# Gate and up projections by seven block products, with sums of weights on VectorE, and down products placed between them

## The chip, the cores and the metric

The kernel runs on one core of a Trainium2 chip. A core has TensorE for matmuls, VectorE, ScalarE and GpSimd for work on elements, and queues that move data; SyncE's queue brings in all weights here. The metric is the device time of one execution in microseconds. Each engine takes its instructions in order and waits on semaphores where it needs another engine's result.

## The reference

A decoder trunk of two layers runs over one sequence of 512 tokens, width 1024. Each layer is a feed-forward step with half weight, an attention (stick-breaking in the first layer, sliding window in the second), and a second feed-forward step; each begins with an RMS norm. All is float32.

```python
def swiglu(h, w_gate_up, w_down):
    gate, up = jnp.split(h @ w_gate_up, 2, axis=-1)
    return (jax.nn.silu(gate) * up) @ w_down
...
    x = x + 0.5 * swiglu(rms_norm(x, norm_gains[i, 0]), ffn_w_gate_up[i, 0], ffn_w_down[i, 0])
    h = rms_norm(x, norm_gains[i, 1])
    ...
    x = x + 0.5 * swiglu(rms_norm(x, norm_gains[i, 2]), ffn_w_gate_up[i, 1], ffn_w_down[i, 1])
```

The inner width of a feed-forward layer is 2816, 22 columns of 128 for gate and as many for up.

## The kernel before, in words

The work is six stages, "0s12w3": FFN0, stick-breaking attention, FFN1, FFN2, window attention, FFN3. The state x lies transposed in eight tiles of 128 features by 512 tokens. A float32 product is made from numbers split into a high and a low part: `terms` (with `mm`, L77) issues three matmuls per tile of 128 x 128 weights, high by high, high by low, low by high. The low part of x is made in `norm_tile` (ScalarE L255, VectorE L256).

Weights come in units of 128 x 1024 (512 KB) into three raw buffers. ScalarE casts a unit to its high part (L183), then VectorE subtracts to get the low part (L188); there are three buffers for split weights, and a unit's buffer is opened again when its last matmul has read it. The order of units is fixed by `queue`.

A feed-forward stage first runs all 22 columns of gate and up: per column two units, each 8 x 3 matmuls of 512 tokens into one bank. Then `swiglu` multiplies both by `rbc`, the inverse norm of each token broadcast to all partitions (L308, L310), applies silu on ScalarE (L309), multiplies (L311) and splits the result (L314, L315). After the last column, eight outputs of 22 x 3 matmuls follow (`dn`); each is added into x (L301) and normed for the next stage.

`rbc` is made while the first units run. After the first unit `norm_rows` sums the squares on TensorE (`ss`) and VectorE computes `nv` and then `nr` by three rounds of small operations on 128 x 4. After the second unit `norm_bcast` spreads it: ScalarE and VectorE make diagonals (`dgh`, `dgl`, L294), two matmuls make `bc`, and VectorE copies it to `rbc` (L298).

Only TensorE's instructions keep the order in which the code is written:

```python
self.scalar, self.vector, self.gpsimd, self.sync = nc.scalar, nc.vector, nc.gpsimd, nc.sync
self.tensor = _Ordered(tc, nc.tensor)
```

A scheduler fixes the order on the other engines when the program is built, by when it reckons the inputs are there; on the chip each engine then keeps to it.

Of the kernel before, what the change touches and what calls it, by code (L numbers as in the profile page):

```python
# [15 lines left out]
P = 128  # L16
# [6 lines left out]
DOWN = (8, 7, 7)  # L23
# [85 lines left out]

class _Trunk:  # L110
    def __init__(self, tc, pools, psum, aps):
        self.tc, self.nc = tc, _Engines(tc)
        self.const, self.work = pools
        self.psum = psum
        self.aps = aps
        self.units = []
        self.raw, self.ready = [], []
        self.taken = self.spent = 0
        self.roped = False
        self.extra = -1  # L120
# [8 lines left out]
    def terms(self, out, pairs, first=True, last=True, release=()):  # L129

# [3 lines left out]
        for i, ((wh, wl), (xh, xl)) in enumerate(pairs):  # L134
# [27 lines left out]
    def _open(self, n):
        size = self.units[n][1]
        hi = self.work.tile([P, size], F32R, tag="whi", name=f"whi{n}", bufs=UNITS)
        lo = self.work.tile([P, size], F32R, tag="wlo", name=f"wlo{n}", bufs=UNITS)
        self.ready.append((hi, lo))

    def advance(self, hi, lo):

        n = self.extra = len(self.ready)  # L170
        self.ready.append((hi, lo))
        self._part(n)
        self._load()

    def _part(self, n, i=0, pieces=1):
        nc, (ap, size, pool) = self.nc, self.units[n]
        size //= pieces
        s = slice(i * size, (i + 1) * size)
        hi, lo = self.ready[n]
        raw = self.raw[n]  # L180
        if pieces > 1:
            nc.sync.dma_start(raw[:, s], ap[:, s])
        nc.scalar.copy(hi[:, s], raw[:, s])  # L183
        if pool and pieces == 1:
            for t in (slice(0, size // 2), slice(size // 2, size)):
                nc.gpsimd.tensor_sub(lo[:, t], raw[:, t], hi[:, t])  # L186
        else:
            nc.vector.tensor_sub(lo[:, s], raw[:, s], hi[:, s])  # L188

    def release(self, count):  # L190
        self.spent += count
        ahead = UNITS + (self.spent <= self.extra)
        while count and len(self.ready) < min(self.spent + ahead, len(self.units)):
            n = len(self.ready)
            self._open(n)
            self._part(n)
            self._load()

    def weights(self, a):

        hi, lo = self.ready[self.taken]
        self.taken += 1
        h3, l3 = (t.rearrange("p (a b) -> p a b", a=a) for t in (hi, lo))
        return [(h3[:, i, :], l3[:, i, :]) for i in range(a)]


    def setup(self, which):
# [823 lines left out]
```

## Time and profile before

| | us |
|---|---|
| median of 3 runs shown (1910.4 to 1915.54) | 1911.14 |
| the profiled execution | 1910.23 |
| its span | 1908.4 |
| FFN1, gate/up (634.10 to 875.09) | 240.99 |
| FFN1, down (875.09 to 994.77) | 119.68 |
| FFN2, gate/up (994.77 to 1235.54) | 240.77 |
| FFN2, down (1235.54 to 1355.30) | 119.76 |

The span runs from the first instruction to the last on the core; the execution's own time has 1.8 us around it. The limits of the stretches are the starts and ends of pieces in the chain of work that ended last. In such a chain each piece is followed by what it released; where it stays on one engine for hundreds of instructions, that engine set the time there. An engine's busy share is of the whole span; the table by stretches gives it for one stage. In rows of a timeline the bracket at the end is the engine's idle time ahead of the instruction and who ended it. Matmuls overlap, so the time of one in a timeline is longer than the distance between two starts.

### The profile page before, as it was taken

What the parts mean: (1) busy time and instruction counts of PE and PEld (TensorE: products, weight loads), DVE (VectorE), ACT (ScalarE), POOL (GpSimd) and SP (SyncE); (2) the same over time, 40 slices, a digit from 0 to 9 for tenths busy, and PEclk for the clock granted to TensorE, in tenths of its full rate; (3) what the DMA queues carried; (4) which work ended last, traced back from release to release, by engine and by line L of the source; (5) the groups of instructions that cost most, each with busy time, mean ns of one, the idle gap of its engine ahead of it and who ended that gap; (6) DMA issues with size and microseconds to landing.
All of it is one profiled execution on the core that took longest, in us unless ns stands there. A gap on an engine that the chain in (4) does not pass through costs nothing.

```text
span 1908.4 us, 22581 instructions
## 1 busy us (share of the span) xinstructions
PE 1877.3 (98%) x8994; PEld 1562.6 (82%) x8994; DVE 970.3 (51%) x1535; ACT 695.6 (36%) x1071; POOL 172.3 (9%) x131
## 2 busy tenths in 40 slices
PE   9999999999999999999999999999998999999999
PEld 7888888877887888888888888888887888888887
DVE  7444433378887644443335444432588664444322
ACT  5322222266665333222223332222357542233221
POOL 1000001233320000000100000001142210000000
PEclk9999999999999999999999999999999999999999
DMA  5323333321122322333333223333221022223331
GB/s 168 98 100 100 94 94 93 106 67 56 46 66 67 100 89 99 100 97 92 98 100 98 90 100 100 94 91 102 82 67 34 28 95 99 93 96 99 97 117 62
DMA packets 49929, 170.52 MB, mean 89 GB/s; under 512 B 5920, under 2 KB 6176, under 8 KB 49824
## 3 DMA queue, kind: packets, MB, share of 16 engines
q1 hardware_dynamic: 49824, 169.07, 28.0%
q8 instruction: 71, 1.16, 0.2%
q14 instruction: 34, 0.28, 0.0%
HBM read 166.96 MB, written 2.10 MB: 89 GB/s over the span
## 4 chain that ended last, share of the span: by engine, by line
PE 85%; DVE 7%; issue 4%; ACT 3%; POOL 1%; DMA 0%; SPq 0%; ACTq 0%; DVEq 0%; POOLq 0%
PE gu L77 49%; PE dn L77 23%; PE op L77 4%; PE tok L77 3%; DVE keep L460 2%; PE pv L77 1%; DVE beta L461 1%; DVE qs L377 1%; PE q L77 1%; DVE wt L483 1%; PE sc L77 1%; PE z L77 1%; ACT keep L454 1%; PE ptr L77 0%; DVE e L793 0%
## 5 line engine op out<-in xcount | busy, mean ns | idle before, releaser
L183 ACT CAST whi<-raw 128x1024 fp32r<-128x1024 f32 (+2 forms) x323 | 330.3, 1023 | 949.3 <-issue 358.0
L77 PE MATMUL gu<-xh,whi 128*128 128x512 f32 x1400 | 545.5, 390 | 1.2 <-ACT whi L183 1.2
L77 PE MATMUL gu<-xh,wlo 128*128 128x512 f32 x1400 | 545.0, 389 | 0.7 <-DVE wlo L188 0.7
L77 PE MATMUL gu<-xl,whi 128*128 128x512 f32 x1400 | 544.8, 389 | 0.5 <-DVE xl L256 0.5
L188 DVE TENSOR_TENSOR wlo<-raw,whi 128x1024 fp32r<-128x1024 f32 (+2 forms) x293 | 349.1, 1192 | 239.6 <-ACT whi L183 236.7
L77 PEld LDWEIGHTS gu<-xh,whi 128*128 128x128 f32 x1400 | 262.9, 188 | 56.2 <-ACT whi L183 1.8
L77 PEld LDWEIGHTS gu<-xh,wlo 128*128 128x128 f32 x1400 | 262.8, 188 | 56.0 <-DVE wlo L188 1.9
L77 PEld LDWEIGHTS gu<-xl,whi 128*128 128x128 f32 x1400 | 262.9, 188 | 55.6 <-DVE xl L256 0.9
L77 PE MATMUL dn<-hh,whi 128*128 128x512 f32 x704 | 273.9, 389 | 0.0
L77 PE MATMUL dn<-hl,whi 128*128 128x512 f32 x704 | 273.9, 389 | 0.0
L77 PE MATMUL dn<-hh,wlo 128*128 128x512 f32 x704 | 273.9, 389 | 0.0
L310 DVE TENSOR_TENSOR u<-gu,rbc 128x512 f32<-128x512 f32 x87 | 60.1, 691 | 274.7 <-PE gu L77 274.7
L77 PEld LDWEIGHTS dn<-hh,whi 128*128 128x128 f32 x704 | 132.1, 188 | 27.7
L77 PEld LDWEIGHTS dn<-hh,wlo 128*128 128x128 f32 x704 | 132.1, 188 | 27.4
L77 PEld LDWEIGHTS dn<-hl,whi 128*128 128x128 f32 x704 | 132.1, 188 | 27.2
L308 DVE TENSOR_TENSOR g<-gu,rbc 128x512 f32<-128x512 f32 x88 | 60.8, 691 | 176.5 <-PE gu L77 176.4
L264 POOL TENSOR_TENSOR acc<-acc,sq 128x512 f32<-128x512 f32 x30 | 46.6, 1553 | 1106.0 <-ACT sq L263 1106.0
L186 POOL TENSOR_TENSOR wlo<-raw,whi 128x512 fp32r<-128x512 f32 x60 | 87.5, 1483 | 163.7 <-ACT whi L183 163.7
L77 PE MATMUL tok<-whi,xh 128*128 128x256 f32 x288 | 85.9, 298 | 0.0
L77 PE MATMUL tok<-whi,xl 128*128 128x256 f32 x288 | 81.9, 284 | 0.1
L77 PE MATMUL tok<-wlo,xh 128*128 128x256 f32 x288 | 81.8, 284 | 0.1
L301 DVE SCALAR_TENSOR_TENSOR x<-dn,x 128x512 f32<-128x512 f32 x32 | 22.1, 692 | 110.9 <-PE dn L77 110.9
(310 smaller groups left out, 1950.3 us busy)
## 6 DMA issues: line engine op xcount, KB each, us to landing
raw<-in_gu_dram SPq DMA_DIRECT2D x173, 512.0 KB, 3.3
raw<-in_dn_dram SPq DMA_DIRECT2D x64, 448.0 KB, 3.3
raw<-in_dn_dram SPq DMA_DIRECT2D x32, 512.0 KB, 3.5
raw<-in_sbqk_dram SPq DMA_DIRECT2D x16, 512.0 KB, 3.4
raw<-in_swin_dram SPq DMA_DIRECT2D x10, 512.0 KB, 3.5
raw<-in_sbv_dram SPq DMA_DIRECT2D x8, 512.0 KB, 3.3
raw<-in_sbo_dram SPq DMA_DIRECT2D x8, 512.0 KB, 3.5
raw<-in_swo_dram SPq DMA_DIRECT2D x8, 512.0 KB, 3.4
```

The costliest lines, as they stand in the source:

```text
L77: return self._tc.keep_in_program_order(method(*args, **kwargs))
L183: nc.scalar.copy(hi[:, s], raw[:, s])
L186: nc.gpsimd.tensor_sub(lo[:, t], raw[:, t], hi[:, t])
L188: nc.vector.tensor_sub(lo[:, s], raw[:, s], hi[:, s])
L264: (nc.gpsimd if k < POOL_SQUARES else nc.vector).tensor_add(self.acc, self.acc, sq)
L301: self.nc.vector.scalar_tensor_tensor(self.x[n], ps, factor, self.x[n], ALU.mult, ALU.add)
L308: nc.vector.tensor_mul(g, gu[0], self.rbc)
L310: nc.vector.tensor_mul(u, gu[1], self.rbc)
L377: nc.vector.tensor_sub(out[other, h, :], src[own, :], out[own, h, :])
L454: nc.scalar.activation(keep[:, :, :n], z[:, :, :n], AF.Sigmoid, scale=-0.125)
L460: nc.vector.tensor_tensor_scan(rev, rev, rev, 1.0, ALU.mult, ALU.bypass)
L461: nc.vector.tensor_mul(beta[:, :, : n - 1], beta[:, :, : n - 1], keep[:, :, 1:n])
```

## The change

Gate and up of one column are taken as one product of a 2 x 2 block matrix of weights with a 2 x 2 block matrix of inputs: the weight blocks are gate and up by odd and even tiles of the 1024 features, the input blocks are odd and even tiles by the first and the second 256 tokens. Winograd's form of Strassen's scheme makes it with seven products (`seven`, p from 1 to 7) for eight. Each is 4 tiles x 3 matmuls of 256 columns. Four of the seven read sums of x (`sums_of_x`, made once at each stage's start: four tiles t0 to t3 by ScalarE and VectorE), and four read sums of weights, S1 to S4, which VectorE makes for each column from the raw units (L329, L333, L334). S1 S3 and S2 S4 fill a split buffer each, A22 A11 one, A12 half of one. The first two columns (`PLAIN`) stay as they were, since `rbc` and the sums of x come with them.

The down product is cut by `GROUPS` into six groups of columns (3, 3, 4, 4, 4, 4). A group's eight pieces (one per output tile, a bank of its own, added into x by L471) run between the products of the next group's columns; `ffn_steps` writes that order. The last group's eight pieces come at the end, and only they are followed by the norm. Within a feed-forward stage there are two more raw buffers, two more split ones (`slotx`) and two half ones. The bank names a, b, c hold the products, dn the pieces.

```diff
-DOWN = (8, 7, 7)
+W2 = T // 2
+HALF = KD // 2
+UNIT = KD * P
+PLAIN = 2
+GROUPS = (3, 3, 4, 4, 4, 4)
+MORE_RAWS, MORE_SLOTS, HALF_SLOTS = 2, 2, 2
+HELD = 8
...
+def ffn_steps():
+    steps = [("plain", u) for u in range(2 * PLAIN)]
+    f, last = PLAIN, None
+    for g, size in enumerate(GROUPS):
+        ends = sum(GROUPS[: g + 1])
+        pieces = [("down", g - 1, n) for n in range(KD)] if g else []
+        while f < ends:
+            here = [pieces.pop(0) for _ in range(-(-len(pieces) // (ends - f)))]
+            col = [("seven", p, f) for p in (1, 5, 2, 6, 3, 7, 4)]
+            if last is not None:
+                col.insert(2, last)
+                last = None
+            if not here:
+                last = col.pop()
+            else:
+                col.insert(-1, here.pop())
+                if here:
+                    col.insert(-3, here.pop())
+                while here:
+                    col.insert(-1, here.pop())
+            steps += col
+            f += 1
+    assert last is None
+    return steps + [("down", len(GROUPS) - 1, n) for n in range(KD)]
...
+    def _split(self, n, s=slice(None), load=None):
+        nc = self.nc
+        tiles, kind, reads, pool, _, _ = self.plan[n]
+        hi, lo = (a[:, s] for a in self.ready[n])
+        raws = [self.raws[m] for m in reads]
+        if kind in ("unit", "A22 A11"):
+            src = raws[0][:, s]
+            reads = reads[:1]
+        elif kind == "A12":
+            src = raws[1][:, UNIT // 2 :]
+            reads = reads[1:]
+        else:
+            g, u = (r.rearrange("p (h c) -> p h c", h=2) for r in raws)
+            if kind == "S1 S3":
+                self.sums = self.fp.tile([P, 2, UNIT // 2], F32, tag="sums", name="sums", bufs=1)
+                nc.vector.tensor_add(self.sums, g, u[:, 0:1, :].broadcast_to([P, 2, UNIT // 2]))
+                src = self.sums.rearrange("p h c -> p (h c)")
+            else:
+                nc.vector.tensor_add(u[:, 0, :], self.sums[:, 0, :], g[:, 1, :])
+                nc.vector.tensor_add(u[:, 1, :], u[:, 0, :], u[:, 1, :])
+                src = raws[1]
+        if load is not None:
+            nc.sync.dma_start(src, load)
+        nc.scalar.copy(hi, src)
+        if pool:
+            for h in (slice(0, UNIT // 2), slice(UNIT // 2, UNIT)):
+                nc.gpsimd.tensor_sub(lo[:, h], src[:, h], hi[:, h])
+        else:
+            nc.vector.tensor_sub(lo, src, hi)
...
+    def sums_of_x(self):
+        nc, fp = self.nc, self.fp
+        self.ts = []
+        for m in range(HALF):
+            xg = fp.tile([P, 2, 2, W2], F32, tag="hs", name="xg", bufs=HELD)
+            for i in range(2):
+                k = 2 * m + i
+                g = self.gain[:, self.which * KD + k : self.which * KD + k + 1]
+                nc.scalar.activation(xg[:, i].rearrange("p h t -> p (h t)"), self.x[k], AF.Copy, scale=g)
+            t = fp.tile([P, 4, W2], F32, tag="hs", name="t", bufs=HELD)
+            nc.vector.tensor_sub(t[:, 0, :], xg[:, 0, 0, :], xg[:, 0, 1, :])
+            nc.vector.tensor_sub(t[:, 2, :], xg[:, 1, 1, :], xg[:, 0, 1, :])
+            nc.vector.scalar_tensor_tensor(t[:, 1, :], t[:, 0, :], -1.0, xg[:, 1, 1, :], ALU.mult, ALU.subtract)
+            nc.vector.scalar_tensor_tensor(t[:, 3, :], t[:, 1, :], -1.0, xg[:, 1, 0, :], ALU.mult, ALU.subtract)
+            ts = fp.tile([P, 2, 4, W2], F32R, name=f"t{m}")
+            nc.scalar.copy(ts[:, 0], t)
+            nc.vector.tensor_sub(ts[:, 1], t, ts[:, 0])
+            self.ts.append(ts)
...
+    def seven(self, p, f, tiles):
+        nc, fp = self.nc, self.fp
+        nm = {2: "b", 5: "c", 3: "c"}.get(p, "a")
+        if (nm, f) not in self.cells:
+            tag, bufs = {"a": ("tr", 2), "b": ("pv", 1), "c": ("z", 1)}[nm]
+            self.cells[nm, f] = self.psum.tile([P, T], F32, tag=tag, name=nm, bufs=bufs)
+        ps = self.cells[nm, f][:, :W2]
+        first = p in (1, 2, 5)
+        for m, (n, i) in enumerate(tiles):
+            wh, wl, used = self.tile(n, i)
+            xh, xl = self.operand(p, m)
+            for j, (l, r) in enumerate(((wh, xh), (wh, xl), (wl, xh))):
+                nc.tensor.matmul(
+                    ps, l, r, start=(first and m == j == 0), stop=(m == HALF - 1 and j == 2), skip_group_check=not first,
+                )
+        if p in (1, 6, 5):
+            r = self.cells[f"r{p}", f] = fp.tile([P, W2], F32, tag=f"r{p}", name=f"r{p}", bufs=2)
+            nc.scalar.copy(r, ps)
+        elif p == 2:
+            g = self.cells["g", f] = fp.tile([P, T], F32, tag="g", name="g", bufs=2)
+            nc.vector.tensor_add(g[:, :W2], ps, self.cells["r1", f])
+        elif p == 3:
+            g = self.cells["g", f]
+            nc.vector.tensor_add(g[:, W2:], ps, self.cells["r6", f])
+            nc.vector.tensor_mul(g, g, self.rbc)
+            nc.scalar.activation(g, g, AF.Silu)
+            nc.vector.tensor_mul(g, g, self.rbc)
+        elif p == 7:
+            h = self.cells["h", f] = fp.tile([P, T], F32, tag="h", name="h", bufs=2)
+            nc.vector.tensor_add(h[:, W2:], ps, self.cells["r5", f])
+            nc.vector.tensor_mul(h[:, W2:], h[:, W2:], self.cells["g", f][:, W2:])
+        else:
+            h = self.cells["h", f]
+            nc.vector.tensor_mul(h[:, :W2], ps, self.cells["g", f][:, :W2])
+            self.keep(f, h)
+            for key in [k for k in self.cells if k[1] == f]:
+                del self.cells[key]
+        self.used(n, HALF)
...
+            self.plain(steps[: 2 * PLAIN], first)
+            last = len(GROUPS) - 1
+            tail = [s for s in steps if s[0][:2] == ("down", last)]
+            for step, tiles in steps[2 * PLAIN : len(steps) - len(tail)]:
+                if step[0] == "seven":
+                    self.seven(step[1], step[2], tiles)
+                    if rope and step[1:] == (7, NF // 2):
+                        self.rope_tables()
+                else:
+                    self.down(step[2], step[1], tiles, None)
+            banks = {}
+            for n in range(2):
+                banks[n] = self.bank("dn")
+                self.down_terms(banks[n], last, tail[n][1][:-1], 0)
             for n in range(KD):
+                self.down(n, last, tail[n][1], following, banks.get(n))
...
+    def plain(self, steps, first):
+        xs = list(zip(self.xh, self.xl))
+        banks = {}
+        if first:
+            order = [(k, u) for k in range(HALF) for u in range(UNITS)] + [(k, u) for u in range(UNITS) for k in range(HALF, KD)]
+            order += [(k, UNITS) for k in range(KD)]
+        else:
+            order = [(k, u) for u in range(2 * PLAIN) for k in range(KD)]
+        for k, u in order:
+            if u not in banks:
+                banks[u] = self.psum.tile([P, T], F32, tag="z", name="gu", bufs=1) if u == UNITS else self.bank("gu")
+            self.mm3(banks[u], [(self.tile(*steps[u][1][k]), xs[k])], first=(k == 0), last=(k == KD - 1))
+            if (u, k) == ((1, KD - 1) if first else (0, KD - 1)):
+                self.norm_rows()
+            if (u, k) == ((UNITS, 4) if first else (1, KD - 1)):
+                self.norm_bcast()
+            if k == KD - 1 and u == (3 if first else 1):
+                self.swiglu(0, (banks[0], banks[1]))
+                self.sums_of_x()
+            if k == KD - 1 and u == 3:
+                self.swiglu(1, (banks[2], banks[3]))
+    def down_terms(self, ps, g, tiles, at):
+        f0 = sum(GROUPS[:g])
+        for j, (n, i) in enumerate(tiles, at):
+            self.mm3(ps, [(self.tile(n, i), self.hs[f0 + j])], first=(j == 0), last=(j == GROUPS[g] - 1))
+    def down(self, n, g, tiles, following, ps=None):
+        at = GROUPS[g] - 1 if ps is not None else 0
+        ps = self.bank("dn") if ps is None else ps
+        self.down_terms(ps, g, tiles[at:], at)
+        self.residual(n, ps, -0.5)
+        if following:
+            following(n)
```

The order of instructions follows in three places. The first is VectorE at the start of FFN2, from the fifth step behind the sum of squares (`ss`) on; `raw` is a unit as loaded, `slot` (before: `whi`, `wlo`) its two parts, `sums` the sums S1 S3. Before:

```order
L273 TENSOR_TENSOR nt<-nt,nv 128x4
L188 TENSOR_TENSOR wlo_7523<-raw_7429,whi_7522 128x1024
L274 SCALAR_TENSOR_TENSOR nr<-nt,nr 128x4
L272 SCALAR_TENSOR_TENSOR nt<-nr 128x4
L273 TENSOR_TENSOR nt<-nt,nv 128x4
L274 SCALAR_TENSOR_TENSOR nr<-nt,nr 128x4
L272 SCALAR_TENSOR_TENSOR nt<-nr 128x4
L273 TENSOR_TENSOR nt<-nt,nv 128x4
L274 SCALAR_TENSOR_TENSOR nr<-nt,nr 128x4
L294 SCALAR_TENSOR_TENSOR dgl<-ident,nr,dgh 128x128 x4
L298 COPY rbc<-bc 128x512
```

The change, from the same step on:

```order
L443 TENSOR_TENSOR nt<-nt,nv 128x4
L329 TENSOR_TENSOR sums<-raw_9730,raw_9777 128x1024
L343 TENSOR_TENSOR half_9833<-raw_9777,half_9833 128x512
L444 SCALAR_TENSOR_TENSOR nr<-nt,nr 128x4
L333 TENSOR_TENSOR raw_9777<-sums,raw_9730 128x512
L343 TENSOR_TENSOR slot_9828<-sums,slot_9828 128x1024
L442 SCALAR_TENSOR_TENSOR nt<-nr 128x4
L334 TENSOR_TENSOR raw_9777<-raw_9777 128x512
L443 TENSOR_TENSOR nt<-nt,nv 128x4
L329 TENSOR_TENSOR sums<-rawx_9816,rawx_9821 128x1024
L444 SCALAR_TENSOR_TENSOR nr<-nt,nr 128x4
L343 TENSOR_TENSOR half_10013<-rawx_9821,half_10013 128x512
```

Between the small steps on 128 x 4 stand now sums, a half split and whole splits; before, one split stood there.

The second is VectorE in the middle of FFN2 before, one column:

```order
L310 TENSOR_TENSOR u_8240<-gu_8208,rbc_7589 128x512
L311 TENSOR_TENSOR u_8240<-g_8239,u_8240 128x512
L188 TENSOR_TENSOR wlo190_8234<-raw190_8134,whi190_8233 128x1024
L315 TENSOR_TENSOR hl9_8246<-u_8240,hh9_8245 128x512
L308 TENSOR_TENSOR g_8311<-gu_8249,rbc_7589 128x512
L188 TENSOR_TENSOR wlo191_8275<-raw191_8165,whi191_8274 128x1024
```

The change, in a column of FFN0 with two down pieces (x2 and x3 receive them):

```order
L548 TENSOR_TENSOR g_3153<-c_3125,r6_3167 128x256
L549 TENSOR_TENSOR g_3153<-g_3153,rbc_387 128x512
L343 TENSOR_TENSOR slot95_3252<-rawx57_2949,slot95_3252 128x1024
L551 TENSOR_TENSOR g_3153<-g_3153,rbc_387 128x512
L471 SCALAR_TENSOR_TENSOR x2_113<-dn_3185,x2_113 128x512
L554 TENSOR_TENSOR h_3211<-a_3110,r5_3138 128x256
L555 TENSOR_TENSOR h_3211<-h_3211,g_3153 128x256
L343 TENSOR_TENSOR slot96_3259<-raw58_3081,slot96_3259 128x1024
L471 SCALAR_TENSOR_TENSOR x3_114<-dn_3214,x3_114 128x512
L343 TENSOR_TENSOR slotx93_3227<-sums_3228,slotx93_3227 128x1024
L558 TENSOR_TENSOR h_3211<-a_3110,g_3153 128x256
L343 TENSOR_TENSOR slot97_3264<-raw59_3083,slot97_3264 128x1024
```

A column's row of six operations has become some eighteen, of which a dozen are shown; the split of `slotx93` from `sums` stands behind a residual and another split.

The third is TensorE between two units of gate/up before:

```order
L77 MATMUL gu_1164<-xl7_206,whi25_1086 128x512
L77 MATMUL gu_1164<-xh7_205,wlo25_1087 128x512
L77 MATMUL gu_1205<-xh0_136,whi26_1117 128x512
L77 MATMUL gu_1205<-xl0_137,whi26_1117 128x512
L77 MATMUL gu_1205<-xh0_136,wlo26_1118 128x512
```

The change, from the second down piece of a column of FFN0 to the next column's first product:

```order
L85 MATMUL dn_3214<-hs14_2463,slotx91_3102 128x512 x3
L85 MATMUL dn_3214<-hs15_2613,slotx91_3102 128x512 x3
L85 MATMUL dn_3214<-hs16_2781,slotx91_3102 128x512 x3
L85 MATMUL dn_3214<-hs17_2931,slotx91_3102 128x512 x3
L85 MATMUL a_3110<-t0_423,slot87_2946 128x256 x3
L85 MATMUL a_3110<-t1_434,slot87_2946 128x256 x3
L85 MATMUL a_3110<-t2_445,slot87_2946 128x256 x3
L85 MATMUL a_3110<-t3_456,slot87_2946 128x256 x3
L85 MATMUL a_3269<-xh0_133,slotx92_3107 128x256
```

A piece of four terms, then p4 of the column, then p1 of the next; twelve matmuls of p1 on, p5 reads `slotx93`, which takes the place of `slotx91`, read last by the piece shown.

## Rows read from the trace of the kernel before

**Rows 1.** The page: busy us and shares by engine; the chain's shares by line.
```profile
PE 1877.3 (98%) x8994; PEld 1562.6 (82%) x8994; DVE 970.3 (51%) x1535; ACT 695.6 (36%) x1071; POOL 172.3 (9%) x131
...
PE gu L77 49%; PE dn L77 23%; PE op L77 4%; PE tok L77 3%; DVE keep L460 2%; PE pv L77 1%; DVE beta L461 1%; DVE qs L377 1%; PE q L77 1%; DVE wt L483 1%; PE sc L77 1%; PE z L77 1%; ACT keep L454 1%; PE ptr L77 0%; DVE e L793 0%
```

**Rows 2.** The chain in order of time: start us, us, what it was.
```profile
30.71 2.04 PE gus L77 x9
...
382.99 11.53 PE tok L77 x96
...
875.09 119.68 PE dn L77 x528
994.77 5.44 PE gu L77 x24
1000.21 0.79 PE ss L77 x8
...
1007.06 228.48 PE gu L77 x1008
```

**Rows 3.** Two stretches of FFN2: length, busy us (count) by engine, clock, DMA.
```profile
994.77:1235.54 240.77, 240.77 (x1067) 199.47 (x1067) 114.40 (x149) 73.62 (x94) 0.00 (x0) 1.00 0.30 96
1235.54:1355.30 119.76, 119.76 (x531) 99.18 (x531) 39.53 (x43) 33.10 (x40) 8.03 (x6) 1.00 0.33 99
```

**Rows 4.** Groups of instructions by line and form: busy, mean ns, idle before.
```profile
L188 DVE TENSOR_TENSOR wlo<-raw,whi 128x1024 fp32r<-128x1024 f32 x223 | 274.6, 1232 | 140.3 <-ACT whi L183 140.1
L183 ACT CAST whi<-raw 128x1024 fp32r<-128x1024 f32 x253 | 266.1, 1053 | 711.5 <-issue 358.0 <-PE gu L77 267.1 <-PE dn L77 57.5
...
L310 DVE TENSOR_TENSOR u<-gu,rbc 128x512 f32<-128x512 f32 x87 | 60.1, 691 | 274.7 <-PE gu L77 274.7
...
L77 PEld LDWEIGHTS tok<-wlo,xh 128*128 128x128 f32 x288 | 55.3, 192 | 0.4 <-POOL wlo L186 0.3
...
L756 DVE TENSOR_TENSOR q<-tok,qgain 128x256 f32<-128x256 f32 x16 | 6.6, 416 | 6.4 <-ACT qsq L755 6.3
```

**Rows 5.** Timeline of VectorE at FFN2's start: start us, us, instruction, idle before.
```profile
1001.03 0.16 DVE L282 TENSOR_SCALAR nv<-ss 128x4 f32<-128x4 f32 x1 [2.88 <-PE ss L77]
...
1001.84 0.16 DVE L273 TENSOR_TENSOR nt<-nt,nv 128x4 f32<-128x4 f32 x1
1001.91 1.23 DVE L188 TENSOR_TENSOR wlo<-raw,whi 128x1024 fp32r<-128x1024 f32 x1
1003.06 0.15 DVE L274 SCALAR_TENSOR_TENSOR nr<-nt,nr 128x4 f32<-128x4 f32 x1
1003.25 0.16 DVE L272 SCALAR_TENSOR_TENSOR nt<-nr 128x4 f32<-128x4 f32 x1
...
1004.23 0.16 DVE L274 SCALAR_TENSOR_TENSOR nr<-nt,nr 128x4 f32<-128x4 f32 x1
1004.93 1.23 DVE L294 SCALAR_TENSOR_TENSOR dgl<-ident,nr,dgh 128x128 fp32r<-128x128 f32 x4 [0.53 <-ACT dgh L293]
1007.09 0.69 DVE L298 COPY rbc<-bc 128x512 f32<-128x512 f32 x1 [0.94 <-PE bc L77]
1007.70 1.22 DVE L188 TENSOR_TENSOR wlo<-raw,whi 128x1024 fp32r<-128x1024 f32 x1
1008.84 0.68 DVE L308 TENSOR_TENSOR g<-gu,rbc 128x512 f32<-128x512 f32 x1
1009.44 0.68 DVE L310 TENSOR_TENSOR u<-gu,rbc 128x512 f32<-128x512 f32 x1
```

**Rows 6.** Timeline of ScalarE behind FFN2's first unit.
```profile
1000.06 1.05 ACT L183 CAST whi<-raw 128x1024 fp32r<-128x1024 f32 x1 [3.28 <-issue]
```

**Rows 7.** TensorE's timeline in the stick-breaking stage; then a stretch behind it.
```profile
472.26 0.73 PE L77 MATMUL z<-ks,qs 128*128 128x512 f32 x2 [1.44 <-ACT beta L456]
...
473.00:478.00 5.00, 5.00 (x18) 3.74 (x17) 3.99 (x6) 4.34 (x7) 1.03 (x1) 0.66 0.02 3
```

**Rows 8.** Timeline of VectorE at FFN0's start.
```profile
21.20 0.69 DVE L264 TENSOR_TENSOR acc<-acc,sq 128x512 f32<-128x512 f32 x1 [0.70 <-ACT sq L263]
...
24.01 0.16 DVE L282 TENSOR_SCALAR nv<-ss 128x4 f32<-128x4 f32 x1 [0.64 <-PE ss L77]
```

More of the change, by code (lines that the diff above doesn't have):

```diff
@@ L168, in advance @@
[L168 to L204, printed above, removed]
+    def queue(self, ap, pool=False, special=False):
+        n = len(self.loads)
+        self.loads.append((ap, None))
+        self.reads.append(1)
+        self.plan.append((KD, "unit", (n,), pool, None, special))
@@ new lines, in _ring, with _load @@
+    def _ring(self, rings, free, own):
+        best = None
+        for r in rings if own and own == self.stage else rings[:1]:
+            e = r.evicts()
+            if e is None:
+                return r
+            if free(e) and (best is None or e < best.evicts()):
+                best = r
+        return best
+    def _load(self):
+        n = len(self.raws)
+        r = self._ring(self.raw_rings, lambda e: self.reads[e] == 0, self.loads[n][1])
+        if r:
+            self.raws.append(r.take(n, [P, UNIT], F32))
+        return r
@@ new lines, in advance, with used, tile @@
+    def advance(self, hi, lo):
+        n = len(self.ready)
+        assert self.plan[n][5] and self.plan[n][2][0] < len(self.raws)
+        self.ready.append((hi, lo))
+        self.left.append(self.plan[n][0])
+        self._split(n)
+        self.pump()
+    def used(self, slot, tiles):
+        self.left[slot] -= tiles
+        if tiles and not self.left[slot]:
+            self.pump()
+    def tile(self, slot, i, width=1):
+        hi, lo = (a[:, i * P : (i + width) * P] for a in self.ready[slot])
+        return hi, lo, (slot, width)
@@ L207, in setup, with take @@
+    def take(self, count, width=1):
+        out = []
+        for _ in range(count):
+            n, i = self.at
+            out.append(self.tile(n, i, width))
+            self.at = (n, i + width) if i + width < self.plan[n][0] else (n + 1, 0)
+        return out
     def setup(self, which):
@@ L402, in project_pair @@
             ps = self.bank(nm)
-            yield from self.terms(ps, list(zip(self.weights(KD), xs)), release=1)
+            yield from self.terms(ps, list(zip(self.take(KD), xs)))
             if start:
@@ L531, in project_early @@
         for n in range(UNITS):
-            opened.append([self.bank("op"), self.weights(KD), 0])
+            opened.append([self.bank("op"), self.take(KD), 0])
         while True:
```

287 lines of the change are left out of this document (174 added, 113 removed).

## The prediction

> **What bounds the kernel now.** I read the page's busy shares first. TensorE is busy for 1877.3 of 1908.4 us, 98%, and VectorE for half of them [rows 1]. The page's chain of waits names the lines: matmuls of gate and up make 49% of the span and those of down 23% [rows 1], so the four feed-forward layers (FFN0 to FFN3), where all of the change lies, are bound by TensorE. The long chain gives the pace of its pieces: 1008 matmuls of 512 columns take 228.48 us and 528 of the down part 119.68, both 0.2267 us each [rows 2]. The same chain holds a stretch of 96 matmuls of 256 columns in 11.53 us, 0.1201 each [rows 2]; all 96 are the same three-product form that the change uses. Then the table by stretches: in FFN2's gate/up, VectorE works 114.40 of 240.77 us and ScalarE 73.62, in its down part 39.53 of 119.76 [rows 3]. So VectorE has room on average, and the question is whether it has it where the change puts its work.
>
> **What goes from TensorE.** A column of gate/up was 2 x 8 x 3 = 48 matmuls of 512, 48 x 0.2267 = 10.88 us. By seven products it is 7 x 4 x 3 = 84 of 256, 84 x 0.1201 = 10.09. That is 0.79 less; 20 columns in 4 layers make -63.3 us. The down products are as many and as wide as before: per column 24 x 0.2267 = 5.44 us, now between the products (4.08 in the columns that do group 1, pieces of three over four columns). Between two widths of matmul I count no gap, since the chain runs from the broadcast's 512 columns into the 256 ones without a piece of its own for a wait.
>
> The trace shows a weight load of 128 x 128 at 192 ns, longer than the 120 ns from one 256-column matmul to the next [rows 4], so loads and matmuls overlap further than by one pair, and the pace of rows 2 holds in spite of it. The Trainium skill, page "TensorE: Matmul & The Clock Gate", section "Back-to-back issue gap", has a sustained spacing of about 81 ns for 128 columns and 131 for 512, hence a fixed part that a narrower matmul does not shrink; an estimate by a straight line between gives 98 ns for 256, so 84 x 98 = 8.2 us for a column against 48 x 131 = 6.3, dearer by 1.9, or +155 us in all. The trace does not agree on either end: 227 ns for 512, and 120 for 256, little over half.
>
> **What VectorE and ScalarE get in the steady part.** From start to start an operation of 1024 columns takes VectorE 1.14 us (the split at 1007.70, next start 1008.84) and one of 512 columns 0.605 (1008.84 to 1009.44) [rows 5]; one of 256 is 0.416 long against 0.691 for 512 [rows 4], less the same overlap of 0.085, 0.33. A column with a full share of down holds 5 of 1024 (three splits of gate/up weights, one of a down unit, one sum), 8 of 512 (a half split, two sums, two products, hs, two residuals) and 5 of 256: 5.7 + 4.84 + 1.65 = 12.2 us, or 13.8 by whole durations (5 x 1.232 + 8 x 0.691 + 5 x 0.416). TensorE takes 10.09 + 5.44 = 15.53, and 14.17 where pieces have three terms and VectorE correspondingly less. It stays TensorE's, with 12% to spare. ScalarE's casts are 4.5 of 1.053 [rows 4] a column and its other work about as much again shorter, some 7 us.
>
> One wait is tight. In every second column with two down pieces, the buffer for S1 S3 is the one that the second piece has just left; behind it on TensorE stand p4 and the next p1, 24 x 0.1201 = 2.88 us, and then p5 reads it. A cast that waits for a matmul begins about 0.15 us before the chain's end of that matmul (1000.06 against 994.77 + 5.44) [rows 2, 6]; 1.05 for the cast and 1.23 for the subtraction bring it to 2.1. About 0.7 us is left, and on VectorE a residual and a finished split stand just ahead, on ScalarE another cast. Two more ends matter: p4 waits for VectorE's reading of bank a (L554), and a piece of 2.72 us covers that. I count 0 to +15 us for all of it, taking little (0), because both engines have their work queued earlier; behind a late subtraction stand p4's product and hs, which only the down pieces of the next group read.
>
> **What the layers' starts cost.** Here the work is bunched. Take FFN2, times from its first matmul, 994.77. The sum of squares is done and `nv` begins at 6.26 (1001.03) [rows 5]. Before, the chain of small operations and one split were done at 1004.39, 3.4 us on, the broadcast came out of the way at 1007.09 - 994.77 = 12.3, and TensorE never stopped. Now that chain has between its steps two sums and two splits of 1024 and six operations of 512. A small one followed by a dependent one costs 0.20, by a wide one 0.07 (1001.84 to 1001.91) [rows 5]: 0.8 + 0.6 + 4 x 1.14 + 6 x 0.605 = 9.6, so `nr` ends near 15.2. `dgl` starts 0.55 later, and from its start to `rbc` the row gives 2.16: `rbc` at 18.0. TensorE stands at the broadcast, after two units and the sum, at 11.67, and goes on at about 17.5: a stall near 5.7 that was not there.
>
> From 18.0 VectorE owes: `rbc`, g, h and the product (four of 512, with a dependence of 0.2 each), hs after ScalarE's cast, to 22.0; then 16 of 256 (5.3), the four subtractions for t0 to t3 of 1024 (4.6), two splits (2.3) and g and h of column 1 (1.2): 13.4 more, 35.5, and 36.3 to 37.5 with ScalarE's casts between. p5, the second product, reads t3 last, so it ends 3 matmuls after, at 37.9 at most. By TensorE's work alone it would end at 4 x 5.44 + 0.79 + 0.48 + 24 x 0.1201 = 25.9. I take **+12.0**; with no wait at all VectorE's sum is 28.5 from 6.26, which gives +9. Nothing gives this back, since behind it TensorE is the busier engine in each column.
>
> An idle TensorE also loses its clock. At 472.26 it resumes after 1.44 us idle [rows 7], and in the five us from 473 the granted clock averages 0.66 [rows 7], down to the lower level, 1.2 GHz: 5 x 0.34 = 1.7 us. The stall at the broadcast hides its own in the next; the second one's remains: +1.7. FFN2 and FFN3 then cost 13.7 each. FFN1: thirty small operations of the rope table have moved into the same stretch, at 0.07 to 0.20 (2.1 to 6); I take 2.6, so 16.3.
>
> FFN0: VectorE's last sum of squares starts at 21.20 and `nv` at 24.01 [rows 8]. Now two splits, two sums' halves, a sum, a half split and a split stand ahead of `nv` (4 x 1.14 + 3 x 0.605 = 6.4, so 28.3), and three of 1024 and three of 512 within the chain (6.6, to 34.9). `rbc` 2.7 later, 37.6; two columns' eight operations of 512, a split and their waits to 45; x's sums, an hs and a weight sum 11.6 and some 1.5 for ScalarE: t3 at 58.2, p5's end at 58.6. The fourth unit ended at 30.71 + 2.04 = 32.75 [rows 2]; p1 and p5 behind it end at 35.6. That is +23.1, and with the clock 24.8; without any wait +18.5.
>
> **The sum.** Starts: 24.8 + 16.3 + 2 x 13.7 = **+68.5** (47 without waits and clock, 80 with the longer ends). Products: -63.3. Steady waits: 0. Net +5.2 on the profiled execution's 1910.23 gives 1915.4; the median of the runs shown is 0.9 higher, 1911.14, so **1916**. About 0.3%, 5.7 us, is the least that the measurement tells from no change: below 1905.4 is faster, above 1916.9 slower. This forecast lies at that edge; its own range is 1904 to 1928 (starts 57 to 80).
>
> **Rivals.** *A: the weight buffers' turn becomes the bound.* If ScalarE and VectorE serve the S1 S3 buffer in their queues' order, one cast and one wide operation late (1.05 + 1.14 - 0.7 = 1.5), then each of some eight places a layer stops TensorE by 1.5 us, and one more of the kind per column is possible at bank a: 32 x 1.5 = 48 at most, less when only some miss; +20 to +40 above my sum, 1935 to 1955. It decides from 0.7 us of lateness on. For it: the window of 2.88 us against 2.1, engines that work in order. Against: 12% spare on VectorE. 0.2.
>
> *B: the starts cost about half.* If the sums and splits ahead of `nr` are done in the time VectorE waits for `nv` (2.88 us of idle time before it) [rows 5] and the sums of x run while TensorE is still on its third and fourth units, the stall is 5 to 7 in FFN1 to FFN3 and 12 in FFN0: +30 to +35, so 1911.1 - 63.3 + 33 = 1881, and 1880 to 1904 over its spread. For it: the rings are two units deeper, so sums could be due earlier. Against: the order of the instructions is fixed and puts them behind `nv`, and VectorE's sum alone is +9 a layer. 0.27.
>
> *C: seven products are no cheaper.* If the weight load of 192 ns set the pace where three loads in a row differ, a column would be 84 x 0.192 = 16.1 us, +5.2 on before, over 400 us slower. The 256-column stretch has the same loads and denies it: 0.02. A fixed part of the spacing, as the skill's section has it, is the same rival in a milder form and is in that 0.02.
>
> **How the numbers follow.** Forecast 0.51, A 0.2, B 0.27, C 0.02. The forecast's own part falls 0.05 faster, 0.21 same, 0.25 slower; B 0.26 faster, 0.01 same; A and C slower. Together faster 0.31, same 0.22, slower 0.47. The range leaves B's far end and A's far end out: 1888 to 1944.
>
> **What would show it.** Right: in the timeline of FFN2's start, `rbc` 17 to 19 us after the first matmul, an idle TensorE of 5 to 6 us before the broadcast and another before p5 by VectorE's L511, the granted clock at half behind them, and then columns of 15.5 us without gaps; TensorE's busy time down by some 60 us. Wrong: if TensorE's idle time in a steady column is over 0.5 us, with p5's weight load waiting for L343 or L338, it is A; if the first p5 of FFN2 ends before 32, it is B; if 84 matmuls take over 10.5 us without idle time at the full clock, it is C.

## The result and the profile after

The changed kernel takes 1916.88 us (median of 12 runs, 1910.77 to 1918.65) against 1912.07 before (12 runs, 1910.40 to 1915.54): a ratio of 1.0021, 95% interval 1.0012 to 1.0030. Forecast were 1916 and +5.2 on the kernel before; measured is +4.8 between the medians, and +6.6 between the two profiled executions (1916.84 against 1910.23). That is 0.2% slower, clear of the noise, but within the prediction's bound of 0.3% for no change, the outcome to which it gave 0.22, the least of the three.

Two large terms lie behind this small difference. First the page of the changed kernel, busy us by engine, answering to [rows 1]: TensorE is busy for 35 us less, VectorE for 554 more.

```profile
PE 1842.2 (96%) x11874; PEld 1667.3 (87%) x11874; DVE 1524.5 (80%) x2487; ACT 944.9 (49%) x1511; POOL 170.8 (9%) x131
```

Three columns with a full share of down (one each of FFN1, FFN2 and FFN3), as in [rows 3]: length, busy us of TensorE, weight loads, VectorE, ScalarE, GpSimd, then clock, DMA share, GB/s.

```profile
800.07:815.63 15.56, 15.56 (x109) 14.58 (x109) 12.62 (x19) 7.12 (x10) 0.00 (x0) 1.00 0.33 106
1157.46:1173.02 15.56, 15.56 (x110) 14.58 (x109) 12.55 (x19) 7.12 (x10) 0.00 (x0) 1.00 0.33 106
1709.93:1725.49 15.56, 15.56 (x110) 14.58 (x109) 12.66 (x19) 7.11 (x10) 0.00 (x0) 1.00 0.33 105
```

A column of 15.53 us was forecast, with 12.2 to 13.8 on VectorE and some 7 on ScalarE. TensorE has no gap in it. In the chain (start, length, what), p7 with the next p1 is one piece of 24 matmuls, 0.120 us each; the first in each layer closes its start:

```profile
64.28 2.88 PE a L85 x24
...
642.29 5.44 PE gu L85 x24
...
686.51 2.88 PE a L85 x24
...
1001.38 5.44 PE gu L85 x24
...
1043.90 2.88 PE a L85 x24
...
1551.24 5.44 PE gu L85 x24
...
1596.37 2.88 PE a L85 x24
```

By TensorE's work alone it would come 4 x 5.44 + 0.79 + 0.48 + 60 x 0.1201 = 30.2 us after the first matmul. It comes after 44.2, 42.5 and 45.1: 14.0, 12.3 and 14.9 lost. In FFN0 it would stand at 32.75 + 7.2 = 40.0 and stands at 64.28: 24.3. Together 65.5 us are lost at the starts; the products gain 63.3.

Where TensorE waits at the starts of FFN0 (the first two rows), FFN1, FFN2 and FFN3 (its timeline; the bracket is the idle time and who ended it). In FFN0 six more waits of 0.6 to 1.1 us follow within p5, for ScalarE's casts or VectorE's subtractions of the sums of x:

```profile
37.99 0.79 PE L85 MATMUL bc<-dgh,onesr 128*128 128x512 f32 x1 [6.64 <-ACT dgh L463]
...
49.12 0.58 PE L85 MATMUL c<-t,slot 128*128 128x256 f32 x1 [4.08 <-ACT t L510]
...
659.00 0.80 PE L85 MATMUL bc<-dgh,onesr 128*128 128x512 f32 x1 [4.88 <-ACT dgh L463]
...
678.97 2.90 PE L85 MATMUL c<-t,slot 128*128 128x256 f32 x12 [5.51 <-DVE h L490]
...
1018.09 0.79 PE L85 MATMUL bc<-dgh,onesr 128*128 128x512 f32 x1 [4.88 <-ACT dgh L463]
...
1036.43 2.06 PE L85 MATMUL c<-t,slot 128*128 128x256 f32 x12 [2.63 <-DVE h L490]
...
1567.95 0.79 PE L85 MATMUL bc<-dgh,onesr 128*128 128x512 f32 x1 [4.88 <-ACT dgh L463]
...
1587.68 2.90 PE L85 MATMUL c<-t,slot 128*128 128x256 f32 x12 [4.13 <-DVE h L490]
```

Some 42 of the 65.5 us are idle time. The rest, some 23 us, is the lower clock behind the stalls: there the matmuls take longer and TensorE counts as busy. So its busy time in the four layers falls by 38.2 us (1448.2 to 1410.1) and not by the 63.3 of the products. All of FFN2, for which [rows 3] have the two parts before, 360.53 us of length and of TensorE together:

```profile
1001.38:1358.78 357.40, 349.89 (x2316) 323.24 (x2316) 291.69 (x430) 168.85 (x242) 7.20 (x5) 0.99 0.30 98
```

The VectorE side of FFN2's start, answering to [rows 5]:

```profile
1007.64 0.17 DVE L452 TENSOR_SCALAR nv<-ss 128x4 f32<-128x4 f32 x1 [0.38 <-PE ss L85]
...
1008.44 0.16 DVE L443 TENSOR_TENSOR nt<-nt,nv 128x4 f32<-128x4 f32 x1
1008.52 1.22 DVE L329 TENSOR_TENSOR sums<-raw,raw 128x1024 f32<-128x1024 f32 x1
1009.65 0.68 DVE L343 TENSOR_TENSOR half<-raw,half 128x512 fp32r<-128x512 f32 x1
1010.26 0.15 DVE L444 SCALAR_TENSOR_TENSOR nr<-nt,nr 128x4 f32<-128x4 f32 x1
...
1016.51 0.15 DVE L444 SCALAR_TENSOR_TENSOR nr<-nt,nr 128x4 f32<-128x4 f32 x1
...
1019.35 0.69 DVE L468 COPY rbc<-bc 128x512 f32<-128x512 f32 x1 [0.93 <-PE bc L85]
...
1035.61 0.68 DVE L490 SCALAR_TENSOR_TENSOR h<-gu,rbc 128x512 f32<-128x512 f32 x1
1036.21 1.21 DVE L511 TENSOR_TENSOR t<-t,t 128x1024 fp32r<-128x1024 f32 x1
```

The small steps stand 0.7 to 1.8 us apart where most stood 0.2 apart; `rbc` starts 18.0 us after the layer, t3 is done 36.0 us after it, and between `nv` and there VectorE idles for little over 2 us.

### The profile page after: what moved, and what is told of

Read it like the earlier page. It is cut to its first block, busy times and chain, and to the rows that moved or that the text cites. A ratio compares the mean times of both kernels' runs of the same rounds, so it can differ in the third digit from the quotient of the medians.

```text
span 1915.0 us, 29636 instructions
## 1 busy us (share of the span) xinstructions
PE 1842.2 (96%) x11874; PEld 1667.3 (87%) x11874; DVE 1524.5 (80%) x2487; ACT 944.9 (49%) x1511; POOL 170.8 (9%) x131
## 4 chain that ended last, share of the span: by engine, by line
PE 80%; DVE 13%; issue 3%; ACT 3%; DMA 1%; POOL 0%; SPq 0%; ACTq 0%; DVEq 0%; POOLq 0%
PE dn L85 25%; PE a L85 24%; PE c L85 12%; PE b L85 6%; PE op L85 4%; PE tok L85 3%; PE gu L85 2%; DVE keep L722 2%; DVE beta L723 1%; PE pv L85 1%; DVE slot L343 1%; DVE qs L635 1%; DVE t L511 1%; DVE wt L745 1%; ACT keep L716 1%
## 5 line engine op out<-in xcount | busy, mean ns | idle before, releaser
L85 PE MATMUL dn<-hs,slot 128*128 128x512 f32 x1152 | 279.7, 391 | 0.0
L85 PE MATMUL a<-t,slot 128*128 128x256 f32 x1872 | 249.9, 283 | 0.0
L85 PEld LDWEIGHTS a<-t,slot 128*128 128x128 f32 x1872 | 241.5, 192 | 6.5
L85 PEld LDWEIGHTS dn<-hs,slot 128*128 128x128 f32 x1152 | 211.0, 188 | 40.4
L338 ACT CAST slot<-raw 128x1024 fp32r<-128x1024 f32 (+1 forms) x155 | 160.0, 1033 | 152.2 <-PE a L85 55.2
L85 PE MATMUL dn<-hs,slotx 128*128 128x512 f32 x960 | 233.1, 391 | 0.0
L85 PEld LDWEIGHTS dn<-hs,slotx 128*128 128x128 f32 x960 | 175.7, 188 | 33.4
L343 DVE TENSOR_TENSOR slot<-raw,slot 128x1024 fp32r<-128x1024 f32 (+1 forms) x125 | 155.3, 1243 | 10.8 <-ACT slot L338 10.7
L471 DVE SCALAR_TENSOR_TENSOR x<-dn,x 128x512 f32<-128x512 f32 x192 | 131.5, 685 | 36.6 <-PE dn L85 36.3
L85 PE MATMUL a<-t,slotx 128*128 128x256 f32 x1008 | 134.1, 283 | 0.0
L85 PE MATMUL b<-xh,half 128*128 128x256 f32 x640 | 131.9, 288 | 0.0
L434 POOL TENSOR_TENSOR acc<-acc,sq 128x512 f32<-128x512 f32 x30 | 44.2, 1472 | 818.8 <-ACT sq L433 818.8
L85 PE MATMUL c<-t,slot 128*128 128x256 f32 x576 | 83.5, 295 | 21.0 <-DVE h L490 12.3
```

What stands on the lines that cost most here:

```text
L85: return self._tc.keep_in_program_order(method(*args, **kwargs))
L338: nc.scalar.copy(hi, src)
L343: nc.vector.tensor_sub(lo, src, hi)
L434: (nc.gpsimd if k < POOL_SQUARES else nc.vector).tensor_add(self.acc, self.acc, sq)
L471: self.nc.vector.scalar_tensor_tensor(self.x[n], ps, factor, self.x[n], ALU.mult, ALU.add)
```

## The experiments

The theory: what VectorE owes between `nv` and t3 is longer than TensorE's work ahead of p5, and nothing else in the change costs. The rivals: only the order of the `nr` chain costs; or the buffers' turn in the steady columns does (rival A).

**The nr chain first.** Sums and their splits are held back until the diagonals are made.

```diff
-            if self.plan[n][1] != "unit" and own != self.stage:
+            if self.plan[n][1] != "unit" and (own != self.stage or (self.hold and self.plan[n][1] != "A22 A11")):
                 return None
...
                 self.norm_bcast()
+                self.hold = False
+                with self.tc.issue_after(self.last.ins):
+                    self.pump()
```

> The changed kernel with one thing in another order: no sum of weights and no split of a sum is opened until the diagonals (dgl) of the broadcast are made, so VectorE's chain from nv to nr runs alone. Theory (VectorE's total between nv and t3 sets when the first p5 ends): the stall of 4.9 us before the broadcast goes in FFN1 to FFN3 and most of 6.6 us in FFN0, but the sums come behind it, ahead of t3, and the wait before p5 grows by nearly as much; 0 to 2 us less per layer, so 1909 to 1917. Rival (the order of the nr chain is the price): 4.9 us of stall and 2.2 us at the lower clock go in each layer and nothing comes back: 1917 - 28 = 1889.

1900.35 us (ratio to the kernel before 0.9942, 0.9925 to 0.9958): between the two. The stall before the broadcast is gone in all four layers, and the wait before p5 has grown (FFN2):

```profile
1007.13 0.39 PE L85 MATMUL bc<-dgh,onesr 128*128 128x512 f32 x1
...
1027.62 2.90 PE L85 MATMUL c<-t,slot 128*128 128x256 f32 x12 [7.57 <-DVE h L491]
```

p5 starts 32.3 us after the layer for 35.2, 2.9 less. Two things in VectorE's timeline account for most of it: two sums of 512 columns (L333 and L334 of the changed kernel) now come behind t3 instead of ahead of it (1.2 us), and VectorE, with wide work at hand, no longer waits for `bc` (0.93 us) and for ScalarE's cast of `hs` (0.69). The profiled spans differ by 17.5 us: the layers give 2.3, 3.8, 2.3 and 5.2 of it, and the window attention, whose code is the same, 4.1 (last section). So the order does cost something by itself, 13.6 us in the four layers, more than the theory's 0 to 8 and half of the rival's 28; most of the stall came back as a longer wait before p5.

**One sum of x for four.**

```diff
             self.ts.append(ts)
+            break
+        self.ts *= HALF
```

> The changed kernel with the sums of x made for one of the four pairs of tiles and used for all (12 operations of 256 columns, 3 subtractions and 3 casts of 1024 and 6 scalings less at each start; this part of the result is left out). Theory (VectorE's total): 12 x 0.33 + 3 x 1.14 = 7.4 us less VectorE work ahead of p5, so the second stall and its clock go and the first stays: 5 us less in FFN2, 7 in FFN1 and FFN3, 7 to 9 in FFN0, some 27 in all: 1886 to 1896. Rival (the order of the nr chain is the price): the first stall is untouched and p5 waits for little: within 5 us of 1917.

1889.73 us, ratio 0.9883 (0.9868 to 0.9897), inside the theory's range. The stall of 4.88 us before the broadcast stays in FFN1 to FFN3, and p5 waits no more there. The rival's "within 5 us" falls: VectorE's work behind the broadcast counts too, and 7.4 us less of it give 25.8 us in the four layers of the profiled executions, 6.4 a layer.

**No sums of weights.**

```diff
-                nc.vector.tensor_add(self.sums, g, u[:, 0:1, :].broadcast_to([P, 2, UNIT // 2]))
-                src = self.sums.rearrange("p h c -> p (h c)")
+                src = raws[0]
...
-                nc.vector.tensor_add(u[:, 0, :], self.sums[:, 0, :], g[:, 1, :])
-                nc.vector.tensor_add(u[:, 1, :], u[:, 0, :], u[:, 1, :])
```

> The changed kernel without the sums of weights: the splits read the raw units themselves (L329, L333, L334 left out, so this part of the result is). Theory (VectorE's total counts at the starts, nothing in the steady part): 2 x 1.14 + 4 x 0.605 = 4.7 us less at each start, with the clock 5 to 6, so 1893 to 1899, and the steady columns keep 15.56 us. Rival A of the prediction (buffers' turn in the steady part): columns get shorter than 15.56 and the time falls by over 30.

1895.44 us, ratio 0.9911 (0.9897 to 0.9926). 2.3 us a column taken off VectorE, 188 us in all, give 21 us. Between the profiled executions the four layers give 20.0 us and the window attention 5.2 (last section). The layers' gain lies at the starts: from p7 to p7 the steady columns take 15.56 us as in the changed kernel. The stall before the broadcast falls to 0.3 to 0.5 us, and p5 waits 5.3 to 6.6 us in FFN1 to FFN3. Rival A's 30 are not there.

**More work for VectorE in the steady columns.** On the changed kernel, four and eight idle operations per column:

```diff
             nc.vector.tensor_mul(g, g, self.rbc)
+            idle = fp.tile([P, T], F32, tag="idle", name="idle", bufs=1)
+            for _ in range(4):
+                nc.vector.tensor_sub(idle, g, self.rbc)
```

> The changed kernel with four idle operations of 512 columns on VectorE in each of the 20 columns of seven products (2.4 us a column). Theory (the steady column has 15.56 us of TensorE and 12.6 us of VectorE): 15.0 still fits, so a column keeps 15.56 and the time moves by 0 to 15 (columns of the first groups, which have 14.2): 1917 to 1932. Rival A of the prediction (one late operation of 1.1 us already stops p5 in every second column): over 1945.

> As the run before with eight idle operations, 4.8 us a column. Theory: VectorE's 17.4 us for a column becomes the pace: 1.9 us a column in those with 15.56 and 3 or so in those with 14.2, less what the depth of the buffers gives at the ends: 80 x 2 = 160 more, 2050 to 2090. If VectorE can put work off across columns for long, less.

1925.28 us (1.0073, 1.0058 to 1.0088) and 2090.04 (1.0929, 1.0913 to 1.0945), the first inside the theory's range, the second at its upper end, 2.2 us a column. Stretches of FFN1, of four and of eight. In the first TensorE is busy all but 0.5 us. In the second VectorE is busy for 95.39 us and TensorE, which now waits for it in many columns and runs part of the rest at the lower clock (0.95), for 94.97.

```profile
860.00:1000.00 140.00, 139.50 (x926) 128.45 (x925) 125.39 (x185) 62.12 (x89) 4.01 (x3) 1.00 0.29 95
```

```profile
900.00:1000.00 100.00, 94.97 (x626) 88.20 (x625) 95.39 (x148) 37.67 (x56) 0.00 (x0) 0.95 0.29 94
```

With four, the first waits of rival A's kind show: once in each layer, in a column of 14.2 us, p4 waits 1.1 to 1.3 us for VectorE's reading of bank a (L557 here, L554 in the changed kernel), and in two layers p5 waits 0.3 to 0.4 us for a split buffer. So 2.4 us a column are about what VectorE has to spare there:

```profile
141.52 1.69 PE L85 MATMUL a<-t,slot 128*128 128x256 f32 x12 [1.27 <-DVE h L557]
```

**Idle matmuls in the stalls**, which keep TensorE's clock: before the broadcast alone, and before p5 too.

```diff
+        for _ in range(fill):
+            self.mm(bc, self.onesr, self.xh[0], start=True, stop=True)
         for n, t in enumerate((hi, lo)):
             self.mm(bc, self.onesr, t.rearrange("p b t -> p (b t)"), start=(n == 0), stop=(n == 1))
...
+        if p == 5 and f == PLAIN:
+            b = self.cells["b", f] = self.psum.tile([P, T], F32, tag="pv", name="b", bufs=1)
+            for _ in range({"0": 26, "1": 32, "2": 20, "3": 26}[self.stage]):
+                self.mm(b, self.onesr, self.xh[0], start=True, stop=True)
```

> The changed kernel with 20 idle matmuls of 512 columns (28 in FFN0) in front of the broadcast, which fill the first stall so that the clock is kept. The prediction's term: the first stall's clock hides in the wait before p5, since that wait ends when VectorE does: within 2 us of the changed kernel, 1915 to 1919. Rival: the clock costs by itself, 2.2 us a layer: 1908.

> As the run before, and 20 to 32 idle matmuls of 512 columns in front of the first p5 too. The prediction's term of 1.7 us for the clock behind the second stall: 1.7 x 4 less than the changed kernel, 1908 to 1912. Rival: that clock costs nothing either, 1915 to 1919.

1914.87 us (ratio to before 1.0012, 1.0002 to 1.0023) and 1908.57 (0.9978, 0.9969 to 0.9987). The first kept FFN1 at 359.0 us (359.1 in the changed kernel) and the wait before its p5 grew from 5.51 to 5.79; its four layers together are 1.4 us shorter, and its median 2.0 below the changed kernel's, with intervals that overlap. The second is 8.3 us below the changed kernel by the medians; by the profiled executions its layers are 0.7, 0.9, 2.0 and 2.5 us shorter, 6.1 together, so one to two us a layer. The same stretches of the changed kernel and of the one with both stalls filled:

```profile
1018.00:1024.00 6.00, 5.91 (x14) 4.66 (x15) 4.14 (x8) 2.48 (x6) 0.00 (x0) 0.51 0.11 44
1037.00:1041.00 4.00, 4.00 (x24) 4.00 (x23) 2.85 (x4) 0.89 (x2) 0.00 (x0) 0.57 0.00 0
```

```profile
1018.00:1024.00 6.00, 6.00 (x28) 4.98 (x27) 4.98 (x12) 4.35 (x8) 0.00 (x0) 1.00 0.01 3
1037.00:1041.00 4.00, 4.00 (x36) 4.00 (x35) 3.51 (x8) 1.64 (x3) 0.00 (x0) 1.00 0.00 0
```

**Three plain columns.** `PLAIN = 3` and their swiglu, nothing else.

> The changed kernel with three plain columns for two (PLAIN = 3): 0.79 us more TensorE work per layer, but 10.9 us more of it stand ahead of the first p5. Theory (VectorE's total ahead of t3, 28.5 us from nv, against TensorE's work ahead of p5): the wait before p5 (2.6 to 5.5 us, with its clock 4 to 8) goes in FFN1 to FFN3 and most of some 12 us in FFN0; the stall of 4.9 us before the broadcast stays. 4 to 6 us less in FFN1 to FFN3, 8 to 10 in FFN0: 1888 to 1898. Rival (only the order of the nr chain): the stall before the broadcast is the price, so 4 x 0.79 more, 1920.

1883.61 us (0.9850, 0.9834 to 0.9866), 4 us better than the range. p5 of FFN1 to FFN3 waits no more; beyond the theory, the scheduler put fewer sums into the `nr` chain, and the stall before the broadcast fell from 4.88 to 2.31.

**The start in another order**, in three steps. First the sums of x ahead of all sums of weights but S1 S3 of the first column:

```diff
+        self.gains_of_x()
...
                 self.norm_bcast()
+                self.limit = base + 2
+                with self.tc.issue_after(self.last.ins):
+                    self.pump()
+                if not first:
+                    self.swiglu(0, (banks[0], banks[1]))
+                with self.tc.issue_after(self.last.ins):
+                    self.sums_of_x()
+                with self.tc.issue_after(self.last_t.ins):
+                    self.limit = base + 4
+                    self.pump()
...
+                with self.tc.issue_after(self.last_t.ins if not first else self.last.ins):
+                    self.swiglu(1, (banks[2], banks[3]))
```

> The changed kernel with the starts in another order: ScalarE scales x at the start of the layer; VectorE runs the nr chain alone, then the sum S1 S3 of the first column, the broadcast, column 0's product, all sums of x, and only behind t3 the other sums of weights and column 1's product; the fourth unit of FFN1 to FFN3 has a bank that p5 does not need. Theory (VectorE's total ahead of t3): from nv 2.2 of small operations, two splits 2.3, dgl 1.2, S1 S3 with its split and half split 2.9, rbc and column 0 3.0, sums of x 9.9: 21.5 for 28.5, so p5 of FFN2 ends near 28.5 us for 37.1 and both stalls but 2 to 3 us go: 8 to 10 less in FFN1 to FFN3, 10 in FFN0: 1877 to 1885. Rival (only the order of the nr chain): 1889.

1888.91 us (0.9882, 0.9867 to 0.9897): short of the range. In FFN2 p5 waits 0.5 to 0.9 us per tile and p6 another 1.1 for its weights, whose sums now come behind t3; in FFN0 p5 waits 13.8 us for column 1's product, whose bank (tag z) it takes, and which stood behind t3:

```profile
49.38 2.90 PE L85 MATMUL c<-t,slot 128*128 128x256 f32 x12 [13.78 <-DVE h L491]
...
1019.49 0.62 PE L85 MATMUL c<-t,slot 128*128 128x256 f32 x3 [0.88 <-DVE t L520]
...
1025.30 1.45 PE L85 MATMUL a<-t,slot 128*128 128x256 f32 x10 [1.08 <-DVE slot L344]
```

> The start in the new order of the run that put the sums of x first, together with three plain columns, and with the splits of units 5 and 6 behind the broadcast. Theory: neither stall is left in FFN1 to FFN3 but 1 us or so, each layer near 344.5 + 0.8 + 1; FFN0's wait before p5 (13.8 us there) shrinks by 10.9. Against 1888.9 that is 5 less in FFN1 to FFN3 and 10 in FFN0: 1860 to 1870. If the steady part held a cost of its own (rival A of the prediction), it would show now as idle time in the columns, and the time would stay above 1875.

1892.13 us (0.9895, 0.9882 to 0.9909), a miss: 22 us above the range. No column idles, but the last plain units do, in FFN0, FFN1, FFN2 and FFN3, for the banks of a product that I had put behind the sums of x:

```profile
45.25 0.79 PE L85 MATMUL gu<-xh,slotx 128*128 128x512 f32 x1 [10.48 <-DVE g L495]
...
668.57 0.76 PE L85 MATMUL gu<-xh,slot 128*128 128x512 f32 x1 [5.07 <-DVE g L495]
...
1021.35 0.47 PE L85 MATMUL gu<-xh,slot 128*128 128x512 f32 x1 [3.66 <-DVE g L495]
...
1565.66 0.77 PE L85 MATMUL gu<-xh,slot 128*128 128x512 f32 x1 [3.66 <-DVE g L495]
```

With both products in their turn:

```diff
-                if not first:
-                    self.swiglu(0, (banks[0], banks[1]))
+                self.swiglu(0, (banks[0], banks[1]))
...
-                with self.tc.issue_after(self.last_t.ins if not first else self.last.ins):
-                    self.swiglu(1, (banks[2], banks[3]))
+                self.swiglu(1, (banks[2], banks[3]))
```

> The run with the new order of the start and three plain columns waited for a bank: there column 1's product (and column 0's in FFN0) stood behind the sums of x, and the last plain units had no bank (TensorE idle by DVE g, 3.7 to 10.5 us a layer). Here both products come when their units are done, the rest is the same. Theory (VectorE's total ahead of t3, now with every bank free in time): no stall over 1 us in FFN1 to FFN3, 3 to 4 us in FFN0: 1855 to 1866. If the total itself were still too long: a wait before p5 by L526 and 1870 to 1885.

**1867.72 us**, ratio 0.9762 (0.9745 to 0.9780), 1.7 above the range and the best of all. FFN1, FFN2 and FFN3 (the first three rows) now take what TensorE's work asks and 1.2 to 2.3 us more. That work is two plain columns, the sum of squares and the broadcast, 20 columns of seven products and the down products, 21.76 + 0.79 + 0.45 + 201.8 + 119.68 = 344.5, and 0.8 for the third plain column: 345.3. FFN0 (the last row) is taken from a point where part of its first units has run; there TensorE still idles 6.0 us (345.27 less 339.29), all of it between 36 and 58 us:

```profile
629.82:977.38 347.56, 346.60 (x2279) 318.75 (x2278) 290.48 (x468) 167.06 (x240) 7.21 (x5) 1.00 0.31 101
977.38:1323.84 346.46, 346.46 (x2280) 318.78 (x2278) 286.00 (x421) 165.89 (x237) 7.20 (x5) 1.00 0.30 101
1515.51:1862.40 346.89, 346.62 (x2279) 318.58 (x2277) 277.68 (x410) 156.03 (x222) 0.00 (x0) 1.00 0.30 99
19.70:364.97 345.27, 339.29 (x2242) 312.01 (x2242) 282.70 (x416) 163.07 (x234) 12.45 (x9) 1.00 0.30 99
```

## Why the prediction was right, point by point

- **Products, -63.3 us**: right. 256 columns keep 0.120 us among themselves with weight loads of 192 ns, as [rows 2, 4] had it; rival C falls. The sign "TensorE's busy time down by some 60 us" did not come: it is 35, because the starts' lower clock adds some 23 us of busy time in the layers and the window attention 4.6. The prediction counted neither.
- **Starts, +68.5**: 65.5. FFN0 24.3 for 24.8, FFN1 14.0 for 16.3, FFN2 12.3 for 13.7, FFN3 14.9 for 13.7. `rbc` at 18.0 is exact, the stall before the broadcast 4.9 for 5.7, p5's end in FFN2 37.1 for 37.9. The reason given for p5's wait was not the first one in FFN1 to FFN3: p5 waited for column 1's L490, whose bank it takes, and L511 stands just behind that in VectorE's queue (1035.61 and 1036.21 in FFN2), so the time is nearly the same. FFN3 stands above FFN2 in part because VectorE waits there 1.42 us for ScalarE's cast of a sum of x (ahead of 1584.24), a wait that FFN2 does not have. The sum of 9.6 us leads to 15.9 and not to 15.2: it counts a sixth operation of 512 that stands behind `nr`, as it did on the chip (`nr` at 15.1, `dgl` at 15.9), so `rbc` comes out right.
- **Clock, +1.7 behind the second stall, none behind the first**: right in kind. By the two runs with idle matmuls the first stall's clock costs 0.4 us a layer or nothing, and both together 1.5 (layers of the profiled executions) to 2.1 (medians).
- **Steady waits, 0**: FFN0 to FFN3 changed by +9.1, -1.4, -3.0 and -0.5 us (359.42 for 350.31, 359.09 for 360.51, 357.40 for 360.44, 359.96 for 360.5), +4.2, of which the starts and products are +2.2; 0.5 a layer is left, which is what columns of 15.56 for 15.53 make in 20 columns (0.6). The tight buffer in FFN0: cast at 293.72, subtraction to 296.02, p5 at 296.39. 0.4 us were left, where I had 0.7:

```profile
293.72 1.05 ACT L338 CAST slotx<-sums 128x1024 fp32r<-128x1024 f32 x1 [1.69 <-PE dn L85]
...
294.80 1.22 DVE L343 TENSOR_TENSOR slotx<-sums,slotx 128x1024 fp32r<-128x1024 f32 x1 [0.39 <-ACT slotx L338]
...
296.39 1.60 PE L85 MATMUL c<-t,slotx 128*128 128x256 f32 x12
```

- **The sum**: within 1 us, partly by luck. The terms were 3 us off at the starts and 2 in the columns, the stick-breaking stage gave 1.1 back, and the window stage, which the prediction did not touch, added 3.6. Between the profiled executions the forecast of +5.2 met +6.6; the 0.9 us that the forecast adds to come from the profiled execution to the median took up most of that, while after the change the two agree (1916.84 and 1916.88).

## What to carry to other kernels

Price a saving on the bound engine and the bunched work of its helpers separately: an engine with 20% to spare in every steady column can still owe 28 us within 19 of the other's work at a phase's start. Before giving a change up, move the helper's work by when it is needed, or put more of the bound engine's plain work ahead of the first need (here both together: 49 us between the changed kernel and the last). When work is put off, look which bank its operand holds: two products left behind put-off sums cost 24 us (1892.13 against 1867.72).

## What the runs showed that was not expected

The window attention, whose order on TensorE is the same in all kernels, took 188.9 us before, 192.5 after, 188.3 with the chain first and 191.7 in the last kernel. TensorE's busy time in it goes along (174.2, 178.7, 172.7 and 177.7 us for the same 1130 rows), and the granted clock is 0.95, 0.93, 0.96 and 0.94. Over all the runs here the stage takes 186.9 to 194.1 us and TensorE is busy in it for 171.4 to 180.3, so several us of a comparison can come from how long it spends at the lower clock. VectorE's order in it does not explain this: by the names in the trace it is the same in the changed kernel, the one with the chain first and the last one. Each figure is from one execution, and twelve executions of the changed kernel alone lie between 1910.77 and 1918.65. Whether the stage differs from kernel to kernel or from execution to execution is therefore not shown.
